# Last feed-forward half of a two-layer diffusion backbone: the first pair of up projections multiplies x·(1 + scale), and the norm's factor and the shift's product are applied to the result

## The chip, the cores and the metric

One Trainium2 chip, one of its cores. The metric is the device time of one execution in microseconds (us); the kernel before has three runs, 1758.97, 1759.12 and 1761.3 us, so a median of 1759.12 us.

## The reference

Two layers work on 256 latent tokens x and 256 context tokens z, 1024 wide. Each layer is a half-step feed-forward, a token mixing and a second half-step feed-forward; the mixing of the last layer gives no context output, and its last feed-forward runs on the latent tokens alone. What the change touches is that last half:

```python
def rms_norm(x):
    return x * lax.rsqrt(jnp.mean(x * x, axis=-1, keepdims=True) + EPS)
def modulate(h, shift, scale):
    return h * (1.0 + scale) + shift
def swiglu(h, w1, w3, w2):
    return (jax.nn.silu(h @ w1) * (h @ w3)) @ w2

x = x + mx[5] * (mix_x @ w_out[l])
x = x + 0.5 * mx[8] * swiglu(modulate(rms_norm(x), mx[6], mx[7]), ffn2_w1[l], ffn2_w3[l], ffn2_w2[l])
```

`mx[6]` and `mx[7]` are the shift and the scale, one number for each of the 1024 features (no dependence on the token). The norm's factor is one number for each token. The hidden width of the feed-forward is 2816, that is 22 blocks of 128.

## The kernel before

**Tiles.** x lies transposed in eight tiles `X[d]`, 128 features by 512 tokens (256 latent, 256 context), fp32. A fp32 product is made of three matmuls of half-precise parts: both operands are split into a high part (a cast) and a low part (the difference), and `mm3` (L281) adds hi·hi, hi·lo and lo·hi into PSUM; all of them are issued from `product`, L272. The activations' parts are `hh{d}` and `hl{d}`, eight pairs from `split_tiles` (L254), the same buffers wherever a normed x or a mixing output is multiplied.

**Weights.** They come from HBM in pieces of 512 KB through the SP queue into `raw` (three buffers). `w_conv` (L228) makes `whi` (ScalarE cast, L235) and `wlo` (VectorE subtract, L238), four buffers each. So the piece after the next four is converted into a buffer that matmuls are still reading, and its cast waits for the last of them.

**The norm.** `norm_square` (L286) squares each X tile as it is written (ScalarE, L288 for d = 0, then L296) and adds the squares into `ss` (GpSimd, L299). `norm_stat` (L306) sums over the features with matmuls by a column of ones (L311, and L313 for the last tile where it was not merged into `ss`), takes the mean on VectorE (`ms`, L319) and the power -1/2 on GpSimd (`rs`, L321). `norm_bcast` (L326) transposes the factor over all partitions into the PSUM tile `pb` (L328). `norm_apply_` (L341) then makes for each d: `htmp` = X·(1+scale)·factor (VectorE, L348), `hh` = cast of htmp + shift (ScalarE, L350), and `hl`: for even d on VectorE (L355), for odd d on GpSimd (L353) after a second pass of ScalarE (L352).

**Lags.** Where both streams are normed, `lag` and `lag2` put the norm's small matmuls five or six products behind (a product is one `mm3`, three matmuls), so that other matmuls run meanwhile. The last half has one stream only: `lag` is None, nothing is merged, and the order on TensorE is output projection, norm, feed-forward.

**The feed-forward** (`ffn`, L385). Each of 22 blocks f has two up projections (`p1`, `p3`: 8 products, so 24 matmuls each), then `finish` makes silu(p1)·p3 and splits it into `gh` and `gl`; the down projections `py` follow. The blocks f = 0 and f = 1 are issued as one group: f = 0 in two PSUM tiles of the kind "M", f = 1 in two of the kind "A" (L404 ff), both called `p13`. A block takes two weight pieces, so f = 0 and f = 1 use four.

**Order.** A scheduler places the instructions of each engine at build time from the dependences and from priorities (`tc.high_priority`, L307, L337 and others); the engines then run their own lists in that order and meet by semaphores. `out_proj` multiplies the mixing outputs `mx` (which lie in the same `hh`/`hl` buffers, columns 0 to 255 where the layer is the last) by the output weights: eight tiles `pyo` of 24 matmuls, each added into X (VectorE, L467) and handed to `norm_square`.

Of the kernel before, what the change touches and what calls it, by code (L numbers as in the profile page):

```python
# [29 lines left out]
PR = 50  # L30
# [38 lines left out]
def tile_backbone(ctx: ExitStack, tc: tile.TileContext, a: dict, out: bass.AP):  # L69
    nc = tc.nc  # L70
# [3 lines left out]
    xp = ctx.enter_context(tc.tile_pool(name="stream", bufs=1))  # L74
# [9 lines left out]
    def small(n, name):  # L84
        return sp.tile([P, n], F32, tag=name, name=name, bufs=2 if name[0] in "de" else 8)
# [12 lines left out]
    X = [xp.tile([P, T], F32, name=f"X{d}") for d in range(KD)]  # L98
# [78 lines left out]
    def mcol(l, m, d, s):  # L177
        return mods[l][:, 8 * m + d, s:s + 1]
# [15 lines left out]
    for l in range(2):  # L194
        ffn_units(l, 1)
        for u in ORDER:
# [6 lines left out]
            elif u in "RNQF":  # L203
                name, n = {"F": ("wfou", 2), "R": ("wgr", 2), "N": ("wna", 6), "Q": ("wgqa", 4)}[u]
# [47 lines left out]


    def split_tiles(d):  # L254
        return (xp.tile([P, T], F32R, tag=f"hh{d}", name=f"hh{d}"),
                xp.tile([P, T], F32R, tag=f"hl{d}", name=f"hl{d}"))

    hooks = []
    gate = [None, False]
# [19 lines left out]
    def mm3(ps, w, k, xh, xl, first, last):  # L279
        wh, wl = w[:2]  # L280
        product(((wh[:, k, :], xh), (wh[:, k, :], xl), (wl[:, k, :], xh)), ps, first, last)  # L281
# [76 lines left out]
    def norm_state(l, m, n):  # L358
# [15 lines left out]
        st["apply"] = apply  # L374
        return st


    def down_order(ns, split):
        tail = split if ns > 1 else 0
# [7 lines left out]
    def ffn(l, m, st, n, pool, npool, bg, after, start=None):  # L387
        ns = n // S
        h = st.setdefault("h", {})
        for f0, f1 in ((0, FA), (FA, NF)):  # L390
            G = {}

            def finish(p1, p3):
                sl = pool.tile([P, T], F32, tag="sl", name="sl", bufs=2)
                nc.scalar.activation(sl[:, :n], p1[:, :n], AF.Silu)
                g = pool.tile([P, T], F32, tag="g", name="g", bufs=2)
                nc.vector.tensor_tensor(out=g[:, :n], in0=p3[:, :n], in1=sl[:, :n], op=ALU.mult)  # L397
                gh = pool.tile([P, T], F32R, tag="gh", name="gh", bufs=FA)
                nc.scalar.copy(gh[:, :n], g[:, :n])
                gl = pool.tile([P, T], F32R, tag="gl", name="gl", bufs=FA)  # L400
                nc.vector.tensor_tensor(out=gl[:, :n], in0=g[:, :n], in1=gh[:, :n].bitcast(F32), op=ALU.subtract)
                G[len(G)] = (gh, gl)
                if f0 or len(G) > (SKIP if start else 0):
                    step(bg)  # L404
                    step(bg)

            fs = list(range(f0, f1))
            if f0 == 0:
                ps, ws = {}, {}
                for f in (0, 1):  # L410
                    for j in range(2):
                        ps[f, j] = bank("M" if f == 0 else "A", "p13")
                steps = [(s, 0, KD) for s in range(ns)]
                if start is not None:
                    steps = [(s, k0, k0 + 2) for k0 in range(0, KD, 2) for s in range(ns)]
                for i, (s, k0, k1) in enumerate(steps):
                    if start is not None:
                        start(s, k0, k1)
                    c = slice(s * S, (s + 1) * S)
                    for f in (0, 1):  # L420
                        for j in range(2):
                            if (f, j) not in ws:
                                ws[f, j] = w_next()
                        for k in range(k0, k1):
                            for j in range(2):
                                mm3(ps[f, j][:, c], ws[f, j], k, h[k][0][:, c], h[k][1][:, c],
                                    i == 0 and k == k0, i == len(steps) - 1 and k == k1 - 1)
                        if i == len(steps) - 1:
                            finish(ps[f, 0], ps[f, 1])
                fs = fs[2:]  # L430
            for f in fs:
                w1 = w_next()
                w3 = w_next()
                p1, p3 = bank("M", "p1"), bank("M", "p3")
                for ps, w in ((p1, w1), (p3, w3)):
                    for k in range(KD):
                        mm3(ps[:, :n], w, k, h[k][0][:, :n], h[k][1][:, :n], k == 0, k == KD - 1)
                finish(p1, p3)
            nk = f1 - f0
            held = {}  # L440
            for mt, s0, s1 in down_order(ns, SPLIT if f1 == NF else 0):
                if mt not in held:
                    if mt == KD - 1 and f1 == NF:
                        lead[0] = ltail[0]
                    held[mt] = [w_next(), w_next()]
                ws = held[mt]
                c = slice(s0 * S, s1 * S)
                py = bank("M", "py")
                for kk in range(nk):
                    mm3(py[:, c], ws[kk // (nk // 2)], kk % (nk // 2), G[kk][0][:, c], G[kk][1][:, c], kk == 0, kk == nk - 1)  # L450
                evac(l, m + 2, mt, py, s0, s1)
                if f1 == NF:
                    after(mt, s0, s1)
                if s1 == ns:
                    step(bg)
                    step(bg)
        for _ in bg:
            pass
# [12 lines left out]
    def mixing(l, st, pool, npool):  # L471
        last = l == 1
# [65 lines left out]
        def gates():  # L538
            wh, wl, wf = w_next()
            pg = mmt("pg")  # L540
            for k in range(KD):
                j = 32 * (k % 4)
                nc.tensor.matmul(pg[j:j + 32, :], wf[:, k, :], h[k][0].bitcast(F32), start=k < 4, stop=4 < k)  # L543
            for k in range(KD):
                nc.tensor.matmul(pg[0:32, :], wh[:, k, :], h[k][1], start=False, stop=k == KD - 1)
            gg = big("gg")
            nc.scalar.copy(gg, pg)
            yield
            g["B"] = [big("Bf"), big("Bb")]
            t1, t2 = [], []  # L550
            for dr in range(2):
                pz = bank("A", "pz")
                nc.tensor.matmul(pz, wg[:, dr, :], gg, start=True, stop=True)
                b_ap = vec[:, l, V_BF + dr:V_BF + dr + 1]
                t1.append(big("t1"))
                nc.scalar.activation(t1[dr], pz, AF.Abs, bias=b_ap)
                t2.append(big("t2"))
                nc.vector.tensor_scalar(out=t2[dr], in0=pz, scalar1=b_ap, scalar2=0.0, op0=ALU.add, op1=ALU.min)
            yield
            last_act = None  # L560
            for fn, kw in ((AF.Exp, dict(scale=-1.0)), (AF.Ln, dict(bias=1.0))):
                for dr in range(2):
                    with tc.issue_after(last_act) if last_act is not None else nullcontext():
                        last_act = nc.scalar.activation(t1[dr], t1[dr], fn, **kw).ins
            for dr in range(2):
                B = g["B"][dr]
                nc.vector.tensor_tensor(out=t2[dr], in0=t2[dr], in1=t1[dr], op=ALU.subtract)
                for c in range(4):
                    o_, i_ = B[:, c * P:(c + 1) * P], t2[dr][:, c * P:(c + 1) * P]
                    if dr:  # L570
                        o_, i_ = o_[:, ::-1], i_[:, ::-1]
                    nc.vector.tensor_tensor_scan(out=o_, data0=ones, data1=i_, initial=0.0, op0=ALU.mult, op1=ALU.add)
# [506 lines left out]
    def out_proj(l, mx, n, after):  # L1079
        ns = n // S  # L1080
        held = {}
        for mt, s0, s1 in down_order(ns, SPLITO):
            if mt not in held:
                if mt == KD - 1:
                    lead[0] = ltail[0]
                held[mt] = w_next()
            c = slice(s0 * S, s1 * S)
            py = bank("M", "pyo")
            for k in range(KD):
                mm3(py[:, c], held[mt], k, mx[k][0][:, c], mx[k][1][:, c], k == 0, k == KD - 1)  # L1090
            evac(l, 5, mt, py, s0, s1)
            after(mt, s0, s1)
# [12 lines left out]
    for l in range(2):  # L1105
# [166 lines left out]
```

## Time and profile before

| | |
|---|---|
| runs, us | 1758.97, 1759.12, 1761.3 (median 1759.12) |
| profiled execution, us | 1757.53, its span 1755.7 |
| granted TensorE clock, mean | 0.989 |
| TensorE busy | 1704.3 us, 97% |
| VectorE, ScalarE, GpSimd busy | 1100.3, 666.7, 214.7 us |
| mixing of the last layer ends, last `pyo` matmul starts | 1555.20 us |
| last half's first `p` matmul starts | 1560.42 us |

Times are in us from the start of the span. The page gives for each engine its busy time; a busy TensorE is not one at its peak, since the records of neighbouring matmuls overlap (each lasts 0.28 us and they start 0.12 us apart). `PEclk` is the clock that TensorE was granted, 1.00 for full speed (2.4 GHz) and 0.50 for half (1.2 GHz). The rows on which the prediction rests stand in a section below.

### The profile page before, as it was taken

Reading aid. Unit: us, or ns where it says so; the run is one execution under the profiler, and the core shown is the slowest. Engines: PE = TensorE matmul, PEld = TensorE weight load, DVE = VectorE, ACT = ScalarE, POOL = GpSimd, SP = SyncE. Lnnn points to the kernel's source line nnn. Section 1 sums busy time; section 2 is a strip of 40 time slices with the busy share of each in tenths; the row PEclk is TensorE's granted clock in tenths of the full one; section 3 lists DMA queues with packets and bytes.
Section 4 is the critical chain, followed back from the end, with each engine's and each line's share of the span. In section 5 each row is a group of like instructions: output and inputs, shape, how many; then the busy total and the mean of one; then the engine's idle time right before and its main releaser. Section 6 shows DMA issues by size and latency. Waiting matters only on the chain.

```text
span 1755.7 us, 28056 instructions
## 1 busy us (share of the span) xinstructions
PE 1704.3 (97%) x11190; PEld 1478.9 (84%) x11190; DVE 1100.3 (63%) x1832; ACT 666.7 (38%) x1122; POOL 214.7 (12%) x249
## 2 busy tenths in 40 slices
PE   7999999998989999999999999999999899989999
PEld 5888888887988788888888888888888787889999
DVE  4577877646787558776333478678733468655554
ACT  4422222235656453222222342222223465554443
POOL 1000000022563130000000210000001335120000
PEclk9999999999999999999999999999999899999999
DMA  9555765334221136555332356567523432146664
GB/s 337 189 185 156 221 208 182 110 97 113 85 56 47 65 104 215 180 177 166 102 96 74 110 203 212 168 199 221 167 81 100 87 108 80 52 130 189 184 191 137
DMA packets 92275, 254.04 MB, mean 145 GB/s; under 512 B 17648, under 2 KB 28144, under 8 KB 91760
## 3 DMA queue, kind: packets, MB, share of 16 engines
q1 hardware_dynamic: 90560, 250.93, 47.6%
q8 instruction: 88, 1.44, 0.3%
q10 hardware_dynamic: 1584, 1.32, 0.2%
q14 instruction: 43, 0.35, 0.1%
HBM read 251.16 MB, written 1.05 MB: 144 GB/s over the span
## 4 chain that ended last, share of the span: by engine, by line
PE 88%; DVE 4%; DMA 2%; ACT 2%; issue 1%; POOL 1%; SPq 0%; POOLq 0%; ACTq 0%
PE p L272 48%; PE py L272 24%; PE pt L272 6%; PE pyo L272 3%; DVE wlo L238 1%; DMA biases<-in_na_rpb_dram 1%; PE po L779 1%; PE prT L770 1%; PE sc L747 1%; PE pf L272 1%; PE modps L143 1%; ACT whi L235 1%; DMA raw<-in_wna_dram 0%; PE pa L663 0%; PE pg L543 0%
## 5 line engine op out<-in xcount | busy, mean ns | idle before, releaser
L235 ACT CAST whi<-raw 128x1024 fp32r<-128x1024 f32 (+3 forms) x358 | 339.9, 951 | 868.3 <-PE p L272 300.2
L238 DVE TENSOR_TENSOR wlo<-raw,whi 128x1024 fp32r<-128x1024 f32 (+3 forms) x358 | 398.4, 1115 | 226.5 <-ACT whi L235 219.8
L272 PE MATMUL p<-hl,whi 128*128 128x512 f32 (+1 forms) x1504 | 528.2, 352 | 2.1 <-DVE hl L355 1.4
L272 PE MATMUL p<-hh,wlo 128*128 128x512 f32 (+1 forms) x1504 | 527.4, 352 | 0.0
L272 PE MATMUL p<-hh,whi 128*128 128x512 f32 (+1 forms) x1504 | 525.9, 353 | 1.1 <-ACT hh L350 1.1
L272 PEld LDWEIGHTS p<-hl,whi 128*128 128x128 f32 x1504 | 285.8, 190 | 40.7 <-DVE hl L355 1.6
L272 PEld LDWEIGHTS p<-hh,whi 128*128 128x128 f32 x1504 | 284.6, 191 | 39.7 <-ACT hh L350 1.6
L272 PEld LDWEIGHTS p<-hh,wlo 128*128 128x128 f32 x1504 | 285.8, 190 | 38.0 <-DVE wlo L238 0.2
L168 DVE CUSTOM_DVE_ANT_0 mprod<-wmod,crow 128x1024 f32<-128x1024 f32 x256 | 301.9, 1219 | 0.0
L272 PE MATMUL py<-gh,whi 128*128 128x512 f32 (+1 forms) x764 | 266.4, 350 | 0.0
L272 PE MATMUL py<-gh,wlo 128*128 128x512 f32 (+1 forms) x764 | 265.8, 348 | 0.0
L272 PE MATMUL py<-gl,whi 128*128 128x512 f32 (+1 forms) x764 | 264.1, 346 | 0.0
L299 POOL TENSOR_TENSOR ss<-ss,sq 128x512 f32<-128x512 f32 (+1 forms) x34 | 40.7, 1198 | 1077.4 <-ACT sq L296 1075.9
L397 DVE TENSOR_TENSOR g<-p,sl 128x512 f32<-128x512 f32 (+1 forms) x88 | 54.9, 624 | 180.4 <-PE p L272 180.0
L272 PEld LDWEIGHTS py<-gh,wlo 128*128 128x128 f32 x764 | 143.4, 188 | 20.5
L272 PEld LDWEIGHTS py<-gl,whi 128*128 128x128 f32 x764 | 143.3, 188 | 19.8
L272 PEld LDWEIGHTS py<-gh,whi 128*128 128x128 f32 x764 | 143.5, 188 | 17.7
L272 PE MATMUL pt<-whi,hl 128*128 128x256 f32 x448 | 132.1, 295 | 7.2 <-POOL hl L353 7.1
L272 PE MATMUL pt<-whi,hh 128*128 128x256 f32 x448 | 132.7, 296 | 0.2
L272 PE MATMUL pt<-wlo,hh 128*128 128x256 f32 x448 | 130.6, 291 | 0.0
L467 DVE SCALAR_TENSOR_TENSOR X<-py,mod,X 128x256 f32<-128x256 f32 x112 | 50.3, 480 | 97.4 <-PE py L272 97.4
L272 PEld LDWEIGHTS pt<-whi,hl 128*128 128x128 f32 x448 | 88.1, 197 | 12.0 <-POOL hl L353 8.9
(218 smaller groups left out, 1714.9 us busy)
## 6 DMA issues: line engine op xcount, KB each, us to landing
wmod<-in_wmodt_dram SPq DMA_DIRECT2D x128, 512.0 KB, 3.9
raw<-in_f1w_dram SPq DMA_DIRECT2D x88, 512.0 KB, 4.3
raw<-in_f2w_dram SPq DMA_DIRECT2D x88, 512.0 KB, 4.2
raw<-in_f1w_dram SPq DMA_DIRECT2D x32, 384.0 KB, 3.7
raw<-in_f2w_dram SPq DMA_DIRECT2D x32, 384.0 KB, 3.2
raw<-in_f1w_dram SPq DMA_DIRECT2D x32, 320.0 KB, 2.9
raw<-in_f2w_dram SPq DMA_DIRECT2D x32, 320.0 KB, 2.9
wfirst<-in_wmodf_dram SPq DMA_DIRECT2D x32, 256.0 KB, 6.5
```

The lines of the kernel that those rows point to most:

```text
L143: nc.tensor.matmul(ps[32 * j:32 * j + 32, :P], sc[:, k, :], tile_[:, j * P:(j + 1) * P], start=(k == 0), stop=(k == KD - 1))
L168: nc.vector.tensor_tensor_reduce(out=prod, in0=raw, in1=crow[:, s], scale=1.0, scalar=0.0, op0=ALU.mult, op1=ALU.add, accum_out=acc[:, s, ...
L235: nc.scalar.copy(hi[:, :k * n], raw[:, :k * n])
L238: wlo[0] = nc.vector.tensor_tensor(out=lo[:, :k * n], in0=raw[:, :k * n], in1=hi[:, :k * n].bitcast(F32), op=ALU.subtract).ins
L272: nc.tensor.matmul(ps, w, x, start=first and i == 0, stop=last and i == len(parts) - 1)
L299: (nc.vector if d == KD - 1 else eng).tensor_tensor(out=st["ss"][:, c], in0=st["ss"][:, c], in1=sq[:, c], op=ALU.add)
L397: nc.vector.tensor_tensor(out=g[:, :n], in0=p3[:, :n], in1=sl[:, :n], op=ALU.mult)
L467: nc.vector.scalar_tensor_tensor(out=X[mt][:, c], in0=py[:, c], scalar=mcol(l, m, mt, s), in1=X[mt][:, c], op0=ALU.mult, op1=ALU.add)
L747: nc.tensor.matmul(ps[:, :n], q[:, e, (t % 2) * P:(t % 2 + 1) * P], ks[e][:, T - n:T], start=i == 0, stop=i == 1)
L770: nc.tensor.transpose(pt[:, c * P:(c + 1) * P], pr[e][:, (2 * half + i) * P:(2 * half + i + 1) * P], ident)
L779: last_mm = nc.tensor.matmul(po[64 * e:64 * e + 64, c0:c0 + P], vs[e][4 - nkt + kt], prT[:, (2 * e + i) * P:(2 * e + i + 1) * P], start=kt ...
```

## The change

Only for the last half (`last`). `st2` takes the mixing's own tiles `mx` as its `hh`/`hl`, lag 5 and lag2 4, and merges the last square. Ahead of the output projection `scaled_shift` puts the split shift into two new columns (512 and 513) of these tiles. After each X tile, `scaled_split` writes the split of x·(1+scale) into columns 256 to 511, which the last layer leaves unused. The pair f = 0 then multiplies columns 256 to 513, that is 256 tokens and twice the shift, before the norm is known. `finish` applies the factor and adds the shift's product to the result. All other blocks multiply the normed values as before, from columns 0 to 255.

```diff
     def split_tiles(d):
-        return (xp.tile([P, T], F32R, tag=f"hh{d}", name=f"hh{d}"),
-                xp.tile([P, T], F32R, tag=f"hl{d}", name=f"hl{d}"))
+        return (xp.tile([P, T + 2], F32R, tag=f"hh{d}", name=f"hh{d}"),
+                xp.tile([P, T + 2], F32R, tag=f"hl{d}", name=f"hl{d}"))
...
+    def scaled_shift(st, l, m):
+        for d in range(KD):
+            hh, hl = st["h"][d]
+            for c in (T, T + 1):
+                nc.scalar.copy(hh[:, c:c + 1], mcol(l, m, d, 0))
+                nc.vector.tensor_tensor(out=hl[:, c:c + 1], in0=mcol(l, m, d, 0), in1=hh[:, c:c + 1].bitcast(F32), op=ALU.subtract)
+
+    def scaled_split(st, l, m, d):
+        hh, hl = st["h"][d]
+        x, c = X[d][:, :S], slice(S, T)
+        with tc.high_priority(offset=PR):
+            nc.scalar.activation(hh[:, c], x, AF.Copy, scale=mcol(l, m + 1, d, 0))
+            nc.vector.scalar_tensor_tensor(out=hl[:, c], in0=x, scalar=mcol(l, m + 1, d, 0), in1=hh[:, c].bitcast(F32),
+                                           op0=ALU.mult, op1=ALU.subtract)
...
-            def finish(p1, p3):
+            def finish(p1, p3, scaled=False):
...
+                if scaled:
+                    rb = pool.tile([P, S], F32, name="rb", bufs=1)
+                    nc.scalar.copy(rb, st["pb", 0][:, :S])
+                    b = small(2, "dsh")
+                    for j, p in enumerate((p1, p3)):
+                        nc.vector.tensor_copy(b[:, j:j + 1], p[:, S:S + 1])
+                        nc.vector.tensor_tensor(out=(sl, g)[j][:, :n], in0=p[:, :n], in1=rb, op=ALU.mult)
+                    nc.scalar.activation(sl[:, :n], sl[:, :n], AF.Silu, bias=b[:, 0:1])
+                    nc.vector.scalar_tensor_tensor(out=g[:, :n], in0=g[:, :n], scalar=b[:, 1:2], in1=sl[:, :n], op0=ALU.add, op1=ALU.mult)
...
                     for f in (0, 1):
+                        scaled = f == 0 and ns == 1
+                        c = slice(S, T + 2) if scaled else slice(s * S, (s + 1) * S)
+                        o = slice(0, T + 2 - S) if scaled else c
...
-            out_proj(l, mx, n2, lambda mt, s0, s1: norm_square(st2, npool, mt, s0, s1, nc.gpsimd))
+            if last:
+                st2.update(h=mx, lag=(5,), lag2=(4,), merge=True)
+                scaled_shift(st2, l, 6)
+
+            def after2(mt, s0, s1):
+                norm_square(st2, npool, mt, s0, s1, nc.gpsimd)
+                if last:
+                    scaled_split(st2, l, 6, mt)
+
+            out_proj(l, mx, n2, after2)
```

In the changed kernel the lines have moved: the shift's split is L381 and L382, the scaled split L388 (ScalarE) and L389 (VectorE), X is written at L494, and `finish` runs from L413 (`rb`) over L416 (`dsh`), L417 (both products by rb), L418 (silu) to L419 (g). The lines up to L328 and L341 to L355 keep their numbers. In the lists below X_82 to X_89 are the eight X tiles, and in the changed kernel the pairs hh_14060/hl_14061, hh_14113/hl_14114, hh_14033/hl_14034 and hh_14037/hl_14038 are those of d = 0 to 3, and hh_14224/hl_14225 that of d = 7.

TensorE, from the end of the output projection on. Before (`p_14587` and `p_14588` are the pair f = 0, `p_14589` and `p_14590` the pair f = 1):

```order
7497 L272 MATMUL pyo<-hl_14225,whi 128x256
7498 L272 MATMUL pyo<-hh_14224,wlo 128x256
7499 L311 MATMUL pb<-ones,ss 128x1
7500 L313 MATMUL pb<-ones,sq 128x1
7501 L311 MATMUL pb<-ones,ss 128x1
7502 L313 MATMUL pb<-ones,sq 128x1
7503 L328 MATMUL pb<-cst,rs 128x128 x2
7504 L272 MATMUL p_14587<-hh_14531,whi 128x256
```

The same place in the changed kernel (`p_14573` and `p_14574` are the pair f = 0, `p_14575` the first tile of f = 1, `p_14576` its second; `p_14777` is the first tile of f = 2):

```order
7528 L272 MATMUL p_14573<-hh_14224,wlo 128x258
7529 L311 MATMUL pb<-ones,ss 128x1 x2
7530 L272 MATMUL p_14574<-hh_14033,whi 128x258
...
7536 L328 MATMUL pb<-cst,rs 128x128 x2
7537 L272 MATMUL p_14574<-hh_14231,whi 128x258
...
7548 L272 MATMUL p_14574<-hh_14224,wlo 128x258
7549 L272 MATMUL p_14575<-hh_14060,whi 128x256
...
7552 L272 MATMUL p_14575<-hl_14061,whi 128x256
...
7558 L272 MATMUL p_14575<-hh_14113,whi 128x256
...
7561 L272 MATMUL p_14575<-hl_14114,whi 128x256
```

Between the last `pyo` matmul and the statistics there are now 30 matmuls of f = 0, between these and the transposes 6, and 12 after the transposes; then f = 1 and the first tile of f = 2 come interleaved.

ScalarE, at the same place. Before:

```order
813 L235 CAST whi<-raw 128x1024
814 L296 ACTIVATE sq<-X_89 128x256
815 L350 ACTIVATE hh_14531<-htmp,mod_98 128x256
816 L350 ACTIVATE hh_14537<-htmp,mod_98 128x256
817 L350 ACTIVATE hh_14544<-htmp,mod_98 128x256
818 L352 ACTIVATE htmp<-htmp,mod_98 128x256
```

In the changed kernel:

```order
827 L235 CAST whi<-raw 128x1024
828 L388 ACTIVATE hh_14224<-X_89,mod_98 128x256
829 L296 ACTIVATE sq<-X_89 128x256
830 L235 CAST whi<-raw 128x1024
831 L350 ACTIVATE hh_14060<-htmp,mod_98 128x256
832 L235 CAST whi<-raw 128x1024
833 L350 ACTIVATE hh_14113<-htmp,mod_98 128x256
834 L350 ACTIVATE hh_14033<-htmp,mod_98 128x256
835 L350 ACTIVATE hh_14037<-htmp,mod_98 128x256
836 L352 ACTIVATE htmp<-htmp,mod_98 128x256 x2
```

Two casts of weights (830 and 832, the fifth and sixth piece of the last half) now stand ahead of the normed tiles; they take the buffers of the two pieces of f = 0, so each waits for one tile of that pair.

VectorE, the same place in the changed kernel:

```order
1543 L299 TENSOR_TENSOR ss<-ss,sq 128x256
1544 L416 COPY dsh<-p_14573 128x1
1545 L319 TENSOR_SCALAR ms<-pb 128x2
1546 L238 TENSOR_TENSOR wlo<-raw,whi 128x1024
1547 L348 SCALAR_TENSOR_TENSOR htmp<-X_82,mod_98,pb 128x256
...
1551 L416 COPY dsh<-p_14574 128x1
1552 L355 SCALAR_TENSOR_TENSOR hl_14061<-htmp,mod_98,hh_14060 128x256
1553 L238 TENSOR_TENSOR wlo<-raw,whi 128x1024
1554 L348 SCALAR_TENSOR_TENSOR htmp<-X_86,mod_98,pb 128x256
```

Here too the fifth and sixth `wlo` stand among the norm's operations (before, none stood between `ms` and the last `hl`), and the last sum of squares is VectorE's.

## Rows read from the trace of the kernel before

**Rows 1.** The page: the busy time of each engine, and the chain that ended last, by engine.
```profile
PE 1704.3 (97%) x11190; PEld 1478.9 (84%) x11190; DVE 1100.3 (63%) x1832; ACT 666.7 (38%) x1122; POOL 214.7 (12%) x249
PE 88%; DVE 4%; DMA 2%; ACT 2%; issue 1%; POOL 1%; SPq 0%; POOLq 0%; ACTq 0%
```
**Rows 2.** Stretches of time, TensorE alone: from and to, length, busy time and matmuls begun, granted clock, DMA share, GB/s.
```profile
1530.00:1541.00 11.00, 9.65 (x86) 1.00 0.00 0
1558.00:1562.00 4.00, 2.01 (x8) 0.71 0.68 214
1562.00:1566.00 4.00, 4.00 (x21) 0.50 0.02 4
1600.00:1700.00 100.00, 100.00 (x841) 1.00 0.63 184
```
**Rows 3.** The chain of waits that ended last, from 1553 to 1600 us: start, length, what.
```profile
1554.59 1.22 POOL ss L299
...
1558.11 0.72 POOL rs L321
...
1558.88 0.45 PE pb L328 x2
...
1559.35 0.49 DVE htmp L348
...
1559.86 0.52 ACT hh L350
...
1560.42 39.64 PE p L272 x305
```
**Rows 4.** Timeline of TensorE: start, length, line, operation, tiles, shapes, count, and in brackets the idle time before it with what ended it.
```profile
1555.20 0.28 PE L272 MATMUL pyo<-hh,wlo 128*128 128x256 f32 x1
...
1557.01 0.38 PE L313 MATMUL pb<-ones,sq 128*128 128x1 f32 x2 [0.77 <-ACT sq L296]
1557.25 0.36 PE L311 MATMUL pb<-ones,ss 128*128 128x1 f32 x2
...
1558.88 0.43 PE L328 MATMUL pb<-cst,rs 128*128 128x128 f32 x2 [1.04 <-POOL rs L321]
1560.42 0.80 PE L272 MATMUL p<-hh,whi 128*128 128x256 f32 x2 [1.11 <-ACT hh L350]
...
1566.10 0.41 PE L272 MATMUL p<-hh,wlo 128*128 128x256 f32 x1
1566.31 0.52 PE L272 MATMUL p<-hh,whi 128*128 128x256 f32 x2
1566.66 0.28 PE L272 MATMUL p<-hl,whi 128*128 128x256 f32 x1
1566.78 0.28 PE L272 MATMUL p<-hh,wlo 128*128 128x256 f32 x1
```
**Rows 5.** Timeline of VectorE, same columns.
```profile
1555.52 0.48 DVE L467 SCALAR_TENSOR_TENSOR X<-pyo,mod,X 128x256 f32<-128x256 f32 x1 [0.30 <-PE pyo L272]
1556.67 1.22 DVE L238 TENSOR_TENSOR wlo<-raw,whi 128x1024 fp32r<-128x1024 f32 x1 [0.67 <-ACT whi L235]
1557.88 0.16 DVE L319 TENSOR_SCALAR ms<-pb 128x2 f32<-128x2 f32 x1
1559.35 1.66 DVE L348 SCALAR_TENSOR_TENSOR htmp<-X,mod,pb 128x256 f32<-128x256 f32 x4 [1.31 <-PE pb L328]
1560.92 0.87 DVE L355 SCALAR_TENSOR_TENSOR hl<-htmp,mod,hh 128x256 fp32r<-128x256 f32 x2
```
**Rows 6.** Timeline of ScalarE, same columns.
```profile
1555.59 1.04 ACT L235 CAST whi<-raw 128x1024 fp32r<-128x1024 f32 x1 [1.15 <-DMA raw<-in_f2w_dram]
1556.55 0.41 ACT L296 ACTIVATE sq<-X 128x256 f32<-128x256 f32 x1
1559.86 1.31 ACT L350 ACTIVATE hh<-htmp,mod 128x256 fp32r<-128x256 f32 x3 [2.90 <-DVE htmp L348]
1561.07 0.49 ACT L352 ACTIVATE htmp<-htmp,mod 128x256 f32<-128x256 f32 x1
...
1570.09 1.05 ACT L235 CAST whi<-raw 128x1024 fp32r<-128x1024 f32 x1 [4.90 <-PE p L272]
```
**Rows 7.** Timeline of GpSimd, same columns.
```profile
1561.64 0.75 POOL L353 TENSOR_TENSOR hl<-htmp,hh 128x256 fp32r<-128x256 f32 x1 [2.82 <-ACT htmp L352]
```
**Rows 8.** The mixing of the last layer: a ScalarE copy of two columns, a wait of TensorE in the output projection, and two TensorE products of 129 and 127 columns, of which the second reads its moving operand from column 129 on.
```profile
1517.03 0.17 ACT L986 COPY fy<-pfo 128x2 f32<-128x2 f32 x1
1539.29 0.61 PE L272 MATMUL pyo<-hh,whi 128*128 128x256 f32 x3 [1.24 <-ACT hh L836]
1516.22 0.39 PE L981 MATMUL pfo<-UC,fou 128*128 128x129 f32 x2
1516.44 0.39 PE L982 MATMUL pfo<-UC,fou 128*128 128x127 f32 x2
```
**Rows 9.** Stretches elsewhere in the kernel: from and to, length, busy time and count of TensorE, of its weight loads, of VectorE, ScalarE and GpSimd, granted clock, DMA share, GB/s.
```profile
395.00:399.00 4.00, 1.81 (x13) 1.40 (x12) 4.00 (x6) 1.78 (x6) 1.35 (x2) 1.00 0.60 129
399.00:403.00 4.00, 3.27 (x15) 3.28 (x16) 2.05 (x5) 1.91 (x5) 2.16 (x3) 0.52 0.71 155
411.00:415.00 4.00, 2.25 (x17) 1.84 (x16) 1.73 (x4) 0.87 (x2) 3.60 (x4) 1.00 0.23 24
415.00:419.00 4.00, 3.98 (x26) 2.80 (x25) 3.02 (x3) 1.60 (x3) 2.13 (x3) 1.00 0.02 4
```

More of the change, by code (lines that the diff above doesn't have):

```diff
@@ L391, in ffn @@
             G = {}
-            def finish(p1, p3):
+            def finish(p1, p3, scaled=False):
                 sl = pool.tile([P, T], F32, tag="sl", name="sl", bufs=2)
-                nc.scalar.activation(sl[:, :n], p1[:, :n], AF.Silu)
                 g = pool.tile([P, T], F32, tag="g", name="g", bufs=2)
-                nc.vector.tensor_tensor(out=g[:, :n], in0=p3[:, :n], in1=sl[:, :n], op=ALU.mult)
+                if scaled:
[7 more added lines that the diff above has]
+                    nc.vector.scalar_tensor_tensor(out=g[:, :n], in0=g[:, :n], scalar=b[:, 1:2], in1=sl[:, :n], op0=ALU.add, op1=ALU.mult)
+                else:
+                    nc.scalar.activation(sl[:, :n], p1[:, :n], AF.Silu)
+                    nc.vector.tensor_tensor(out=g[:, :n], in0=p3[:, :n], in1=sl[:, :n], op=ALU.mult)
                 gh = pool.tile([P, T], F32R, tag="gh", name="gh", bufs=FA)
@@ L418, in ffn @@
                         start(s, k0, k1)
-                    c = slice(s * S, (s + 1) * S)
                     for f in (0, 1):
+                        scaled = f == 0 and ns == 1
+                        c = slice(S, T + 2) if scaled else slice(s * S, (s + 1) * S)
+                        o = slice(0, T + 2 - S) if scaled else c
                         for j in range(2):
@@ L425, in ffn @@
                             for j in range(2):
-                                mm3(ps[f, j][:, c], ws[f, j], k, h[k][0][:, c], h[k][1][:, c],
+                                mm3(ps[f, j][:, o], ws[f, j], k, h[k][0][:, c], h[k][1][:, c],
                                     i == 0 and k == k0, i == len(steps) - 1 and k == k1 - 1)
                         if i == len(steps) - 1:
-                            finish(ps[f, 0], ps[f, 1])
+                            finish(ps[f, 0], ps[f, 1], scaled)
                 fs = fs[2:]
@@ L542, in gates @@
                 j = 32 * (k % 4)
-                nc.tensor.matmul(pg[j:j + 32, :], wf[:, k, :], h[k][0].bitcast(F32), start=k < 4, stop=4 < k)
+                nc.tensor.matmul(pg[j:j + 32, :], wf[:, k, :], h[k][0][:, :T].bitcast(F32), start=k < 4, stop=4 < k)
             for k in range(KD):
-                nc.tensor.matmul(pg[0:32, :], wh[:, k, :], h[k][1], start=False, stop=k == KD - 1)
+                nc.tensor.matmul(pg[0:32, :], wh[:, k, :], h[k][1][:, :T], start=False, stop=k == KD - 1)
             gg = big("gg")
```

## The prediction

> **What bounds the kernel now.** I read the page first: TensorE is busy for 1704.3 of the span's 1755.7 us and holds 88% of the chain that ended last [rows 1], so only time in which TensorE stands still or runs at half clock can be won. Then the stretches of time: from 1600 to 1700 us TensorE is busy for 100.00 of 100 at clock 1.00, while from 1558 to 1562 it is busy for 2.01 of 4 and the next 4 us run at 0.50 [rows 2]. Third, the chain of waits through that place: sum of squares on GpSimd, power, transposes, htmp, hh, and then TensorE with nothing between its products up to 1600 [rows 3]. This is the norm between the last output projection and the last feed-forward, and nothing else is there for TensorE to do.
>
> Its price by TensorE's timeline [rows 4]: the last output matmul begins at 1555.20, the next could begin 0.12 later, at 1555.32 (0.12 is the step at full clock, 1566.66 to 1566.78). The first up projection begins at 1560.42: 5.1 us lost. From there to 1566.31 the step is 0.21 (1566.10 to 1566.31), the half level; 28 matmuls take 5.89 us there where they would take 28 x 0.12 = 3.36 at full clock: 2.5 us lost. Together **7.6 us**. Since TensorE has no gap behind it up to the end, the end moves with the moment at which the first matmuls of the feed-forward are done.
>
> **The change, part by part.** It fills the wait with the 48 matmuls of f = 0, which now need x and the scale, but not the norm. I carry the new order forward with times of the rows of before.
>
> *The 30 matmuls ahead of the statistics.* They run from 1555.32 to 1555.32 + 30 x 0.12 = 1558.92. The two extra columns (258 for 256) cost 48 x 0.12 x 2/256 = 0.05 us. The last three need the split of X7. X7 ends at 1556.00 [rows 5]; ScalarE is then in a weight cast until 1556.63 [rows 6]; the scaled cast, priced as the square of the same shape (0.41 [rows 6]), ends at 1557.04. VectorE is in its weight part until 1557.89 [rows 5], and the low part, priced as an hl (0.87 for two [rows 5]), ends at about 1558.3. The 29th matmul reads it at 1555.32 + 28 x 0.12 = 1558.68. So there is no wait, with 0.4 to spare. The other splits come one per output tile and find both engines with room, though X6 and X7 are then written some 0.4 late; 16 operations of 0.41 to 0.44, at nothing. If that cover were gone, 0.4 us would be lost here.
>
> *Statistics.* The last square is merged by VectorE behind the low part, at about 1558.7, before 1558.92. Two matmuls of 0.24 (1557.01 to 1557.25 [rows 4]) lead to 1559.40; the two of the unmerged square, 0.48, are gone. Then 6 matmuls of f = 0 run to 1560.12. Mean: 0.4 after the last statistic began, as before (from 0.23 behind 1557.25 to 1557.88 [rows 4, 5]), so 1559.56 to 1559.72. The shift's copy ahead of it on VectorE, one column, is priced at 0.17 as ScalarE's two-column copy [rows 8]; it waits for the 30th matmul and is over before the statistics are. Power: 0.07 later, 0.72 long [rows 3], so the transposes begin at 1560.56: TensorE waits 0.45. Transposes: 0.45 [rows 3], to 1561.0; 12 matmuls, to 1562.45. Now f = 0 is done.
>
> *What is queued ahead of the normed tiles.* The change adds a wait here. The fifth weight cast now stands ahead of hh0 on ScalarE and the sixth ahead of hh1; before, the first of them came after everything, at 1570.09 [rows 6]. The fifth waits for the first tile of f = 0 (30th matmul, ended at about 1559.05): cast of 1.05 [rows 6] to 1560.1, VectorE's part of 1.22 [rows 5] to 1561.3. Only then comes htmp0, which could have begun at 1561.03 (0.47 behind the transposes [rows 3]): 0.3 late. Four htmp take 1.66 [rows 5], the first 0.49 [rows 3]; hh0 takes 0.52 [rows 3] and is ready at 1562.3, just before TensorE is free. The sixth cast waits for the second tile of f = 0 (1562.6), and runs to 1563.65 with hh1, hh2, hh3 behind it (1.31 for three [rows 6]), to 1564.9, then the second pass of htmp1 (0.49 [rows 6]), to 1565.3, then GpSimd's hl1 (0.75 [rows 7]), to 1566.1. VectorE ends its four htmp at 1562.96, copies the second shift column, and makes hl0 by 1563.5.
>
> *TensorE there.* Three matmuls on hh0 to 1562.81; wait for hl0, 0.7; six matmuls on hl0 and hh0, three on hh1, to 1564.6; wait for hl1, 1.5. Later low parts come every 0.4 to 0.8 us and find a backlog of f = 1 and f = 2, priced at nothing.
>
> *Sum.* Now lost: 0.47 statistics + 0.45 wait + 0.45 transposes + 0.7 + 1.5 + 0.05 for the columns = **3.6 us**, against 7.6: a gain of 4.0, if the clock holds.
>
> *The rest.* 16 ScalarE and 16 VectorE operations of one column make the shift's split, in the mixing; at 0.17 each [rows 8] 2.7 us on each engine, which in most places only fill idle time: bounds 0 and 0.8 later for TensorE, taken as 0.1. The scheduler also moves some output products forward into the end of the mixing. From 1530 to 1541 TensorE is busy for 9.65 of 11 [rows 2], 1.24 of it one wait of an output product for hh [rows 8]. If this wait is filled, 1.3 us is won; if a product comes later, up to 0.8 is lost; I take 0.5 won, near the middle. The new finish of f = 0 (a copy, two products, a silu with bias, 0.4 us each like the operations above) has read its PSUM tiles by about 1570, behind the norm's low parts; f = 3, the first to need them again, begins behind 144 matmuls, at about 1576: nothing. DMA issues are the same, in the same order on SP. In all -4.0 - 0.5 + 0.1 = -4.4 us.
>
> **Against which time.** The profiled execution took 1757.53, so 1753.1; the median of the runs is 1759.12, 1.6 above it. On the median that is **1754.7 us**.
>
> **The rivals.**
>
> *The clock falls in the new thin stretch.* From 1562 to 1566 my chain has TensorE busy for 0.81 + 1.1 = 1.9 of 4 us. Elsewhere, 1.81 busy of 4 was followed by a granted clock of 0.52, and 2.25 of 4 by 1.00 [rows 9]: this stretch lies between. A fall would cost about what it costs now, 2.5 us, and leave a gain of 1.9: **1757.2**. Against it: the gaps are two, with matmuls between, and the 1.24 us wait at 1539 cost no clock: 1.00 from 1530 to 1541 [rows 2, 8]. The Trainium skill, page "TensorE: Matmul & The Clock Gate", Part 1, says that half speed is the default state and that recent activity lifts it; rows 9 agree, with 0.52 behind the thinner and 1.00 behind the denser stretch, and by that rule this rival depends on the moment at which the thin stretch falls.
>
> *The queue eats the gain.* Normed tiles stand behind two weight conversions. If the fifth and sixth piece land later, or X6 and X7 slip and the scaled split with them, hl1 comes 1.5 to 3 us later than 1566.1, and a gain of 1.4 to 2.9 is left, near **1757**. For it: the change puts 2.3 us of conversion (1.05 and 1.22) ahead of a chain that had none. Against it: TensorE has other products up to 1562.45.
>
> *Slower: the width of the tiles.* All 16 tiles grow to 514 columns, 2056 bytes, so every second one may begin 8 bytes off. The kernel has some 6000 matmuls that read them. If each took 1.3 ns more, 8 us would be lost, the gain gone, and the kernel 3.5 us slower: near **1762.7**; it decides from about 0.7 ns each (no gain left). Against it: a product of 127 columns that starts at column 129 takes no longer (0.39) than one of 129 columns that starts at an even one (0.39) [rows 8]. The Trainium skill, page "Advanced Engine Details and Errata", section SBUF Cachelines, says that SBUF has lines of 16 bytes and that going to another line costs; by that rule a shifted row of 256 columns touches 65 lines for 64, an estimate of 1.9 ns per shifted matmul and some 5 us in all. The trace speaks against it, by the row just named.
>
> *It could also win more.* Were hl1 not late and the 1.24 us wait filled, the gain would be 4.0 + 1.5 + 1.2 = 6.7: 1752.4.
>
> **How the numbers follow.** 0.2% is 3.5 us, about what a measurement of this kernel can tell from no change. My forecast, a gain of 3.6 to 6.7, has 0.56, the clock 0.25, the queue 0.12, the width 0.07. Faster by over 0.2%: the forecast and a little of the next two where the mixing gives its 1.3, 0.61. Within: the clock and the queue, less that, 0.30. Slower: the width and some of what the mixing could lose, 0.09. The range goes from 1752.0 (the larger gain, and half of a microsecond between sets of runs) to 1758.4 (the clock falls and the mixing loses 0.8 more than taken, 1757.2 + 1.2); the forecast's own is 1752.4 to 1755.5.
>
> **What would show it.** Matmuls of 258 columns from about 1555 on with no wait ahead of the first; a wait near 0.45 ahead of the transposes; waits of 0.7 and 1.5 for hl0 and hl1; the fifth cast near 1559 and the sixth near 1562.6; clock 1.00 in every stretch from 1555 to 1575. Half clock near 1566 would make the first rival right; a wait for hl1 of over 3 us the second; a longer mean of the matmuls in the first 1500 us, where nothing else has changed, the third.

## The result and the profile after: 11 us slower, and not where the change works

The changed kernel takes 1770.44 us (median of four runs, 1769.21 to 1771.35) against 1759.05 (four runs, 1758.97 to 1761.3): ratio 1.0066, interval [1.0054, 1.0078]. The forecast was 1754.7 in a range of 1752.0 to 1758.4. It was wrong in sign.

At the place that the change is about, the waits came out nearly as forecast. TensorE's waits there, by line waited for (us in total, times, longest), changed kernel, 1572 to 1592 us:

```profile
PE p L272 <- POOL hl L353: 1.4, 1, 1.4
PE p L272 <- DVE hl L389: 0.6, 1, 0.6
PE p L272 <- DVE hl L355: 0.5, 1, 0.5
PE pb L328 <- POOL rs L321: 0.2, 1, 0.2
```

Forecast were, in this order, 1.5, 0, 0.7 and 0.45. The stretches there (columns as in [rows 2], which they answer):

```profile
1574.00:1578.00 4.00, 3.40 (x28) 1.00 0.74 212
1578.00:1582.00 4.00, 3.33 (x26) 1.00 0.66 190
1582.00:1586.00 4.00, 2.59 (x15) 0.80 0.57 184
1586.00:1590.00 4.00, 4.00 (x29) 0.77 0.03 13
```

TensorE is no longer idle for 5 us, and the clock still falls, for a shorter time: the first rival came true in part. From the start of the last output matmul to that of the last matmul of the kernel it is 192.30 us where it was 196.89, but part of these 4.6 us has another cause (below).

The time went elsewhere. Stretches of before, and then of the changed kernel, in parts of the program where both issue the same matmuls (the last line is from the last half):

```profile
100.00:300.00 200.00, 200.00 (x881) 1.00 0.63 192
700.00:900.00 200.00, 200.00 (x881) 1.00 0.50 152
```
```profile
100.00:300.00 200.00, 200.00 (x865) 1.00 0.62 189
700.00:900.00 200.00, 200.00 (x865) 1.00 0.52 155
1600.00:1700.00 100.00, 100.00 (x855) 1.00 0.66 193
```

TensorE is busy all the time in both, at full clock in both, and begins 865 matmuls where it began 881: a 512-column matmul starts later behind the one before it, and nothing waits. In the last half it is the other way round: 855 for 841 [rows 2], so 256-column matmuls follow each other faster. A busy share of 100% hides both. In groups, from 100 to 300 us (line, operation, out<-in, shapes, count, busy us, mean ns of one), before and then changed:

```profile
L272 PE MATMUL p<-hh,wlo 128*128 128x512 f32 x198 | 77.1, 389 | 0.0
L272 PE MATMUL py<-gl,whi 128*128 128x512 f32 x96 | 37.3, 388 | 0.0
```
```profile
L272 PE MATMUL p<-hh,wlo 128*128 128x512 f32 x193 | 75.8, 393 | 0.0
L272 PE MATMUL py<-gl,whi 128*128 128x512 f32 x96 | 37.9, 394 | 0.0
```

Not only the products of the widened hh/hl are slower, but also py, whose gh/gl the change does not touch. The mean distance between starts in unbroken runs of such matmuls is called the step here: p 226.76 ns before and 231.22 after, py 228.96 and 232.59 (232.4 in five of its six stretches, 233.3 in one); in the last half p 120.0 and 116.7. For 2880 and 1404 matmuls of 512 columns that is 12.8 + 5.1 = 17.9 us. By stage (from starts on TensorE's timeline, us, each against before), with the experiments of below:

| kernel | first feed-forward | mixing and output of layer 0 | its second and the next feed-forward | mixing and output of layer 1 | last half |
|---|---|---|---|---|---|
| changed | +7.2 | +0.4 | +10.2 | -0.2 | -4.6 |
| e1, wide tiles alone | +4.7 | +1.1 | +8.0 | +0.6 | -4.1 |
| e2, what lies behind moved | +2.4 | +1.1 | +2.8 | 0.0 | -0.9 |
| e15, change without shift and width | +3.0 | +1.4 | 0.0 | +2.1 | -3.9 |
| e13, change at aligned places | -0.4 | +2.0 | -3.3 | -2.9 | -1.0 |
| e14, e13 and columns from 112 | -0.6 | +2.5 | -3.3 | -1.9 | -6.1 |

The first feed-forward, which waits for its first loads, and the mixings vary by 2 to 3 us between kernels in which they are the same; the last half varies by the clock and by the 256-column step.

### The profile page after: what moved, and what is told of

Its sections match the earlier page's. It is cut to its first block, busy times and chain, and to the rows that moved or that the text cites. A ratio compares the mean times of both kernels' runs of the same rounds, so it can differ in the third digit from the quotient of the medians.

```text
span 1768.7 us, 28103 instructions
## 1 busy us (share of the span) xinstructions
PE 1714.8 (97%) x11186; PEld 1471.0 (83%) x11186; DVE 1108.3 (63%) x1861; ACT 671.9 (38%) x1147; POOL 213.6 (12%) x249
## 4 chain that ended last, share of the span: by engine, by line
PE 87%; DVE 5%; DMA 4%; ACT 2%; issue 1%; POOL 1%; SPq 0%; POOLq 0%; ACTq 0%
PE p L272 48%; PE py L272 24%; PE pt L272 6%; PE pyo L272 3%; DMA biases<-in_na_rpb_dram 1%; DVE wlo L238 1%; PE po L806 1%; PE prT L797 1%; PE pf L272 1%; PE sc L774 1%; ACT whi L235 1%; DMA raw<-in_wna_dram 0%; PE pa L690 0%; DMA raw<-in_f1w_dram 0%; DMA wfirst<-in_wmodf_dram 0%
## 5 line engine op out<-in xcount | busy, mean ns | idle before, releaser
L272 PE MATMUL p<-hl,whi 128*128 128x512 f32 (+2 forms) x1504 | 530.8, 354 | 4.5 <-POOL hl L353 2.1
L272 PE MATMUL p<-hh,wlo 128*128 128x512 f32 (+2 forms) x1504 | 528.2, 353 | 0.3 <-DVE wlo L238 0.3
L272 PE MATMUL p<-hh,whi 128*128 128x512 f32 (+2 forms) x1504 | 525.8, 353 | 1.0 <-ACT whi L235 0.9
L272 PEld LDWEIGHTS p<-hl,whi 128*128 128x128 f32 x1504 | 283.3, 189 | 48.0 <-POOL hl L353 2.5
L272 PEld LDWEIGHTS p<-hh,whi 128*128 128x128 f32 x1504 | 280.9, 188 | 44.5 <-ACT whi L235 1.1
L272 PEld LDWEIGHTS p<-hh,wlo 128*128 128x128 f32 x1504 | 283.3, 189 | 41.5 <-DVE wlo L238 0.6
L272 PE MATMUL py<-gh,wlo 128*128 128x512 f32 (+1 forms) x764 | 267.7, 351 | 0.0
L272 PE MATMUL py<-gl,whi 128*128 128x512 f32 (+1 forms) x764 | 267.7, 351 | 0.0
L272 PE MATMUL py<-gh,whi 128*128 128x512 f32 (+1 forms) x764 | 267.3, 352 | 0.0
L272 PEld LDWEIGHTS py<-gl,whi 128*128 128x128 f32 x764 | 143.9, 188 | 20.8
L272 PEld LDWEIGHTS py<-gh,wlo 128*128 128x128 f32 x764 | 143.8, 188 | 20.8
L272 PEld LDWEIGHTS py<-gh,whi 128*128 128x128 f32 x764 | 143.7, 188 | 20.9
L272 PE MATMUL pt<-whi,hl 128*128 128x256 f32 x448 | 131.6, 294 | 8.7 <-POOL hl L353 8.6
L272 PE MATMUL pt<-whi,hh 128*128 128x256 f32 x448 | 131.6, 294 | 0.2 <-ACT nt L548 0.2
L272 PE MATMUL pt<-wlo,hh 128*128 128x256 f32 x448 | 130.0, 290 | 0.0
L494 DVE SCALAR_TENSOR_TENSOR X<-py,mod,X 128x256 f32<-128x256 f32 x112 | 50.3, 481 | 103.4 <-PE py L272 103.3
L272 PEld LDWEIGHTS pt<-whi,hl 128*128 128x128 f32 x448 | 87.0, 194 | 13.5 <-POOL hl L353 11.5
```

What stands on the lines that cost most here:

```text
L272: nc.tensor.matmul(ps, w, x, start=first and i == 0, stop=last and i == len(parts) - 1)
L494: nc.vector.scalar_tensor_tensor(out=X[mt][:, c], in0=py[:, c], scalar=mcol(l, m, mt, s), in1=X[mt][:, c], op0=ALU.mult, op1=ALU.add)
```

## The experiments

The theory after the result: a matmul's step depends on where its moving operand (the activations' tile that it streams) lies in SBUF, and the wider tiles moved it. Tiles begin at multiples of 32 bytes, so the 2056 bytes of a tile take 2080, hh/hl drift by 32 from tile to tile, and what lies behind moves by 512, by 576 with the new `dsh`. "At 64" below means the tile's first byte modulo 512. Before, the weights whi/wlo and hh/hl lie at 64, gh/gl at 128.

**e1: wide tiles alone.**
```diff
-        return (xp.tile([P, T], F32R, tag=f"hh{d}", name=f"hh{d}"),
-                xp.tile([P, T], F32R, tag=f"hl{d}", name=f"hl{d}"))
+        return (xp.tile([P, T + 2], F32R, tag=f"hh{d}", name=f"hh{d}"),
+                xp.tile([P, T + 2], F32R, tag=f"hl{d}", name=f"hl{d}"))
...
```


> The kernel before with nothing changed but the width of the 16 hh/hl tiles (514 columns; pitch 2080 bytes, since tiles begin at multiples of 32; what lies behind them moves by 512). Its instructions are those of before in the same order. Theory of the place (the wider tiles move the operands of the matmuls, and the 512-column matmuls take 3 to 4 ns more): 1759 + 4428 x 0.0039 = about 1776, step of p in the first 300 us 0.231 for 0.227. Rival (the time is lost in the last mixing or the last half, by the new order): 1759, step 0.227.

1767.78 against 1757.79 (one run each). p's step is 231.3, as in the changed kernel; py's is 229.0, as before, and 512 is a move that leaves the place modulo 512. So ten microseconds come from the width alone, without one instruction of the change. The 1776 counted py's matmuls too, which kept their step, and left out that 256-column steps fall.

**e2: only what lies behind moved, by 576; e3: all hh/hl moved by 32.**
```diff
+    pad = sp.tile([P, 144], F32, name="pad", bufs=1)     # e2
+    pad = xp.tile([P, 8], F32, name="pad")               # e3, ahead of hh0
+    nc.gpsimd.memset(pad, 0.0)
```


> The kernel before with an unused tile of 576 bytes behind the hh/hl tiles: hh and hl lie as before, everything behind them (gh, gl, the mixing's tiles) lies where the changed kernel has it. If the place of each operand counts by itself: p at 0.2268 as before, py at 0.2323 for 0.2289, so 1404 x 0.0034 = 4.8 us more, about 1764. If only the width of hh/hl counts (and py is slowed by something that hh/hl do): 1759. If only what lies behind counts: about 1776.

> The kernel before with an unused tile of 32 bytes ahead of hh0: all hh/hl and what lies behind move by 32 bytes, pitch 2048 as before. If the place of hh/hl relative to the weights' tiles counts: step of p at or near 0.231, up to 1771. If the pitch alone counts (tiles that lie differently to each other): 1759.

e2: 1762.88, 5.1 more than 1757.79, where 4.8 was expected. e3: 1778.51, so a move by 32 bytes costs 20.7 us, more than the 1771 that was expected at most, and worse than the changed kernel, whose tiles lie at all multiples of 32 in turn. Groups of e2, then of e3, same stretch (L274 is L272, moved by the pad's two lines):
```profile
L274 PE MATMUL p<-hh,wlo 128*128 128x512 f32 x195 | 75.9, 389 | 0.0
L274 PE MATMUL py<-gl,whi 128*128 128x512 f32 x96 | 37.9, 395 | 0.0
```
```profile
L274 PE MATMUL p<-hh,wlo 128*128 128x512 f32 x190 | 75.0, 395 | 0.0
L274 PE MATMUL py<-gl,whi 128*128 128x512 f32 x96 | 38.3, 399 | 0.0
```
Each moving operand's own place counts: e2 slows py alone. The pitch (the distance from one tile to the next) is not needed for it: e3 keeps 2048.

**e4: the change without the shift and without the width** (f = 0 multiplies 256 columns; its shift's product is left out); **e15: the same, timed.**
```diff
-        return (xp.tile([P, T + 2], ...
+        return (xp.tile([P, T], ...
...
-                scaled_shift(st2, l, 6)
...
-                        c = slice(S, T + 2) if scaled else ...
+                        c = slice(S, T) if scaled else ...
```


> The changed kernel without the shift in its pair f = 0: hh/hl are 512 wide again, the pair multiplies 256 columns, and the shift's product is left out of f = 0. Everything else of the change stands. Theory of the place: the local gain stays (4.6 us from the last output product to the end, by the traces) and the loss is gone: about 1754.5. Rival (the order costs the time): about 1770 as the changed kernel.

> The changed kernel without the shift in f = 0 and without wider tiles again (the shift's product of f = 0 is left out), timed, since the single run of it stands against a spread of 2 to 3 us. The change's own part, without any move of tiles: 2.1 us by the shorter waits and up to 2.5 us more where the clock does not fall, 1754.5 to 1757, ratio 0.9975 to 0.999.

One run of 1754.99 against 1757.79, then 1757.17 (eleven runs) against 1759.53: ratio 0.9988 [0.9979, 0.9997]. So the early pair itself, without the shift, gains some 2 us on the median (0.5 to 3.7 by the interval), less than my 4.4. In the profiles of e4 and e15, which are one kernel, the last half is 3.9 us shorter and the clock stays up at the thin stretch; in e13, with the same order on TensorE there and nearly the same waits (0.2, 0.5 and 1.4; in e15 0.2, 0.4 and 1.5), it is followed by 0.57. e15, then e13:
```profile
1569.00:1573.00 4.00, 2.10 (x16) 1.00 0.61 154
1573.00:1577.00 4.00, 4.00 (x34) 1.00 0.28 112
```
```profile
1558.00:1562.00 4.00, 2.24 (x17) 1.00 0.56 146
1562.00:1566.00 4.00, 3.85 (x19) 0.57 0.30 118
```
One order, both outcomes: in the profiles of this order the clock stayed up twice without the shift (e4, e15) and fell twice with it (changed kernel, e13). Whether the shift or chance decides it, and how often the clock fell in the runs without a profile, is not shown.

**e5, e6, e7, e10, e11: other places**, by pads of 448, 480 with 32, 64 with 320, 192 and 320 bytes as in e2 and e3; **e9: all moved together**, weights too:
```diff
+    pad = cp.tile([P, 16], F32, name="pad")              # e9, ahead of the weights' tiles
```


> The kernel before with the hh/hl tiles moved by 448 bytes, so that they begin at 0 modulo 512, and gh/gl at 64 (before: 64 and 128; the weights' tiles stay at 64 modulo 512). If the step depends on the place of the moving operand relative to the weights modulo 512 alone, py now takes the step that p had at 64, 0.2268 (256 columns: 0.120), and p at 0 shows a new one. If it depends on something else (which tile it is, the place modulo more than 512), py takes another step than 0.2268.

> The kernel before with hh/hl at 32 modulo 512 and gh/gl at 128 as before. py: 0.2289 as before whatever the rule. p: above 0.2268 if 64, the weights' own place, is the best for it; all starts tried so far that are 32 off a multiple of 64 (96, 160) took 0.233, so 0.233 is expected, and a time near 1776; 1759 if only distance counts and 32 on this side is harmless.

> The kernel before with hh/hl at 128 modulo 512 and gh/gl at 0. If the place modulo 512 alone counts, p takes the step that py had at 128, 0.2289 (2880 x 0.0021 = 6 us more), and py the step that the run with hh/hl at 0 shows for p.

> The kernel before with an unused tile of 64 bytes ahead of the weights' tiles: all of raw, whi, wlo, X, hh/hl, gh/gl move together by 64, so hh/hl lie at 128 modulo 512 and gh/gl at 192, and the weights at 128 too. If the step depends on the distance to the weights: p at 0.2268, py at 0.2289 as before, 1758. If on the place of the moving operand alone: p at 0.2289, py at 0.2333, as those places had with the weights at 64: about 1758 + 6 + 6 = 1770.

> The kernel before with hh/hl at 256 and gh/gl at 320 modulo 512. Both places are new. If 64 is a best place among equals, p and py take 0.2289 or 0.2333 and the time is 1764 to 1778; a place at which the 512-column step is below 0.2268 would show as a time below 1755.

> The kernel before with hh/hl at 384 and gh/gl at 448 modulo 512, the last two multiples of 64. As for 256 and 320: 1764 to 1778 unless one of the places is better than 64.

Times of e5, e6, e7, e9, e10 and e11: 1767.89, 1776.24, 1763.47, 1761.42, 1768.28 and 1764.69, one run each, against medians of 1758.38 (e5 to e7) and 1758.98. Steps in ns, whichever of p or py stood at the place (weights at 64; 256 columns in the last half):

| place modulo 512 | 0 | 32 | 64 | 96 | 128 | 160 | 192 | 256 | 320 | 384 | 448 |
|---|---|---|---|---|---|---|---|---|---|---|---|
| 512 columns, p | 233.3 | 233.3 | 226.8 | 233.3 | 228.9 | | | 233.3 | | 228.9 | |
| 512 columns, py | 233.3 | | 226.7 | | 229.0 (e6: also 233.3) | 233.3 | 233.3 | | 226.7 | | 232.4 |
| 256 columns, p | 113.3 | 118.3 | 120.0 | 116.7 | 117.8 | | | 117.8, then 113.3 | | 117.8 | |
| 256 columns, py | 117.8 | | 119.9 | | 117.8 | 120.0 | 118.7 | | 119.9 | | 118.7 |

For 512 columns p and py agree to 0.1 wherever both stood at one place, but for e6, and places 256 apart agree to 1 (192 and 448 are the pair that differs). In e9 p kept 226.8 and py 229.0 though they lay at 128 and 192: in this one move of all tiles the distance to the weights counts, not the place itself. Its time is 3 us above the 1758 expected, in the first feed-forward and the mixings (+1.7, +1.5 and +1.4), not in the steps. e9's groups, same stretch:
```profile
L274 PE MATMUL p<-hh,wlo 128*128 128x512 f32 x197 | 76.7, 389 | 0.0
L274 PE MATMUL py<-gl,whi 128*128 128x512 f32 x96 | 37.3, 388 | 0.0
```
The place does not settle the step alone. In e6 gh/gl lie at 128 as before, and 228.9 was expected whatever the rule; two of its six stretches of py take 233.3, the other four 228.9. In e10 the 256-column products of p take 117.8 in the first part of the last half and 113.3 in the second, with hh/hl where they were. e6 in two stretches of py alone, then e10 in two of p alone (matmuls begun in brackets):
```profile
170.00:230.00 60.00, 60.00 (x259) 1.00 0.68 207
1165.00:1225.00 60.00, 60.00 (x264) 1.00 0.70 213
```
```profile
1590.00:1630.00 40.00, 40.00 (x342) 1.00 0.68 203
1685.00:1725.00 40.00, 40.00 (x355) 1.00 0.64 194
```
And for 256 columns p and py differ at place 0 (113.3 and 117.8). What chooses between two steps at one place, these runs do not show.

The kernel before had p at the best place for 512 columns and the worst of these for 256.

**e8: no tile moved, the shift by 32 matmuls of two columns.**
```diff
...
+                                        nc.tensor.matmul(psh[:, 2 * j:2 * j + 2], ws[f, j][q][:, k, :], sh[:, k, :], ...)
```


> The changed kernel with 512-wide tiles as before and the shift's product of f = 0 by 32 small matmuls of two columns (shift's high and low part against whi and wlo) into a PSUM tile of its own. No tile moves. Theory of the place: the first 1370 us as before, the last half shorter than before by the 4 us that the run without the shift gained, less what the 32 small matmuls take and no wait hides (32 x 0.06 to 0.12 = 1.9 to 3.8, of which up to 2 in waits): 1755 to 1758. Rival (the change itself is slower): above 1760.

1758.46 (ten runs) against 1758.38: ratio 1.0001 [0.9991, 1.0011], so nothing is left of the gain. Such a matmul takes a step of 0.11 us, nearly as much as one of 256 columns (0.12 here). Two of them on TensorE's timeline:
```profile
1562.58 0.25 PE L464 MATMUL psh<-dgs,wlo 128*128 128x2 f32 x1
1562.69 0.25 PE L464 MATMUL psh<-dgs,whi 128*128 128x2 f32 x1
```
22 of them lie between 1562.55 and 1564.82; then come the two transposes and 12 matmuls of 256 columns, and among these, at about 1566.4, the clock fell, although TensorE had been busy throughout:
```profile
1562.00:1566.00 4.00, 4.00 (x37) 1.00 0.30 116
1566.00:1570.00 4.00, 4.00 (x22) 0.55 0.47 131
1570.00:1574.00 4.00, 4.00 (x23) 0.60 0.37 99
```

**e12: the kernel before, normed values of the last half in columns 112 to 367.**
```diff
+            if last:
+                st2["col"] = 112
...
+            if "col" in st:
+                hh, hl = hh[:, st["col"]:], hl[:, st["col"]:]
```


> The kernel before with one thing changed: in the last feed-forward half the normed values go into columns 112 to 367 of hh/hl and are read there, so that the 256-column matmuls read from 0 modulo 512 (64 + 448) where they read from 64. No tile moves and no instruction is added. Theory of the place: 1056 matmuls at 0.1133 for 0.1200, 7.0 us less: about 1751.5, ratio 0.996. If the place of the tile and not of the columns counts: 1758.5, ratio 1.000.

1753.22 (ten runs, 1748.27 to 1758.90) against 1758.98: 0.9970 [0.9955, 0.9984], near the 0.996. From 1600 to 1700 us:
```profile
1600.00:1700.00 100.00, 100.00 (x874) 1.00 0.65 192
```
874 matmuls for 841 [rows 2], without an instruction more or less.

**e13: the whole change at aligned places; e14: with columns from 112 as well.**
```diff
...
+        return (xp.tile([P, T + 64], F32R, tag=f"hh{d}", name=f"hh{d}"),
+                xp.tile([P, T], F32R, tag=f"hl{d}", name=f"hl{d}"))
...
+            hi, lo = (st["h"][d][0][:, T + j:T + j + 1] for j in (0, 1))
...
+                    nc.vector.tensor_tensor(out=b, in0=bb[:, 0:4:2], in1=bb[:, 1:4:2], op=ALU.add)
```


> The changed kernel with its tiles placed again: hh 576 columns wide (2304 bytes), hl 512, both shift parts in hh's columns 512 and 513 (high and low, added after the products), small tiles in two buffers for eight to make room; hh and hl lie at the weights' own place modulo 256, and so do gh/gl. If the place alone costs the changed kernel its time: p at 0.2268, py at 0.2267, the first 1375 us 2 to 3 us shorter than before (1404 x 0.0022) and the last half shorter by the change's own gain, 2 to 4.5 us as the clock falls or not: 1751 to 1755, ratio 0.996 to 0.998. If the change has a cost of its own: 1759 or above.

> As the last one, and the normed values of the last half in columns 112 to 367, at 0 modulo 256 against the weights: 1008 matmuls of 256 columns at 0.1133 for 0.1200, 6.7 us less again: 1744 to 1748, ratio 0.992 to 0.994. If overwriting the scaled columns makes the normed tiles wait for f = 0, up to 1 us of it is lost.

e13: 1751.85 (five runs) against 1759.53, ratio 0.9954 [0.9940, 0.9967]. e14: 1748.11 (five runs), ratio 0.9936 [0.9923, 0.9948]. Both are faster than the kernel before and the changed one. e13's groups:
```profile
L272 PE MATMUL p<-hh,wlo 128*128 128x512 f32 x199 | 77.4, 389 | 0.0
L272 PE MATMUL py<-gl,whi 128*128 128x512 f32 x96 | 37.3, 389 | 0.0
```
The change is the same and the hh tiles are even wider than in the changed kernel, but hh/hl and gh/gl all lie at the weights' place modulo 256. In e14 the normed values overwrite scaled columns, and the scheduler then puts the rest of f = 0 behind the first products of f = 1: TensorE waits 1.77 us for the last sum of squares and 1.11 for hh0, and the clock falls as before (0.63 and 0.52 from 1557 to 1565), so part of what the early pair gives is lost again. What e14 has over e13 is the 256-column step (113.4 for 120.0 ns over some 1000 matmuls).

## Why the prediction was wrong

- **What bounds the kernel**, the 5.1 us and 2.5 us of [rows 3, 4]: right but for a count. Between 1560.42 and 1566.31 there are 26 matmuls, not 28, so half clock cost 5.89 - 26 x 0.12 = 2.8 us, and the whole price is 7.9 for 7.6.
- **The chain of the new order**: right but for one wait and some sizes. The low part of X7 was priced at 0.44 with 0.4 us to spare; it was 0.6 late. VectorE was the reason, priced at nothing ("both engines with room"): three of the last four scaled low parts took 0.96, and X7 was written 2.3 us after the last output matmul began where it had been 0.3 [rows 4, 5]. Beside each of the three GpSimd's sum of squares was running, beside the fourth, of 0.47, none; no run tests whether that is the reason. VectorE, then GpSimd, then ScalarE:
```profile
1573.05 1.21 DVE L238 TENSOR_TENSOR wlo<-raw,whi 128x1024 fp32r<-128x1024 f32 x1
1574.18 0.96 DVE L389 SCALAR_TENSOR_TENSOR hl<-X,mod,hh 128x256 fp32r<-128x256 f32 x1
1575.07 0.47 DVE L494 SCALAR_TENSOR_TENSOR X<-pyo,mod,X 128x256 f32<-128x256 f32 x1
1576.59 0.47 DVE L389 SCALAR_TENSOR_TENSOR hl<-X,mod,hh 128x256 fp32r<-128x256 f32 x1
...
1574.12 0.74 POOL L299 TENSOR_TENSOR ss<-ss,sq 128x256 f32<-128x256 f32 x1 [1.68 <-ACT sq L296]
...
1577.54 1.05 ACT L235 CAST whi<-raw 128x1024 fp32r<-128x1024 f32 x1 [1.16 <-PE p L272]
...
1580.96 1.05 ACT L235 CAST whi<-raw 128x1024 fp32r<-128x1024 f32 x1 [0.17 <-PE p L272]
```
  The queue on ScalarE was as forecast: the fifth and sixth cast stand ahead of hh0 and hh1, each some 0.8 us later behind the last output matmul than forecast, mostly by the 0.6.
- **The clock** was a rival with 0.25. It fell in the changed kernel (0.80, 0.77) and in e13 (0.57), not in e4 and e15.
- **The step that failed** is the price of the wider tiles. The sum gave them 0.05 us, for two more columns in 48 matmuls, and left the step of every other matmul in the program as it was. The runs showed 17.9 us in the 512-column matmuls, before 256-column ones gave some back, and 10.0 us in all by the width alone (e1). The rival that doubted this term, "Slower: the width of the tiles", had 0.07: right in direction, wrong in mechanism in three points. It thought of tiles "8 bytes off"; they lie at multiples of 32. It looked at the widened tiles alone, while py lost 5.1 us too. And it dismissed the effect by [rows 8], two products of 129 and 127 columns, which are neither fp32r (the type of hh, hl and the weights' parts) nor 512 wide and have other weights: no row for the case in hand. Its size, 1.3 ns on 6000 matmuls, was 4.5 ns on 2880, 3.6 on 1404 and a gain of 3.3 on some 1000. The Trainium skill's rule that I put beside it (page "Advanced Engine Details and Errata", section SBUF Cachelines, 16-byte lines) does not explain it: no operand here begins off a 16-byte line, and a move by 32 bytes of whole lines costs 20.7 us.
- **Neighbouring gain**: of the last half's 4.6 us, e1 has 4.1 without the change, by the 256-column step and a shorter time at half clock. So the profile of after alone would have credited the change with it. The forecast gain of 4.0 showed at its size only where no tile moved and the clock stayed up (3.9 in e4 and e15).
- **The mixing**, -0.5 + 0.1: -0.2 measured, inside what these stages vary by.

What stays open: why the step depends on the distance between moving operand and weights, modulo 256 bytes as far as tried, and what chooses where one place shows two steps. The runs show steps by place, not a mechanism; 224 and the odd multiples of 32 above it were not tried by themselves.

## What to carry to other kernels

A tile that grows by a few bytes moves every tile behind it; before costing such an edit by its instructions, work out where the operands of the busiest matmuls will lie relative to their weights, and put a pad or a padded width there that keeps it. Compare the count of matmuls begun in stretches in which TensorE is 100% busy: that, and not the busy share, shows a slower step. Do not take a matmul of two columns for a small one: with a weight load of its own it cost 0.11 us here, and with 32 of them the whole gain was gone.

## What the runs showed of the hardware that was not expected

- Steps between 226.7 and 233.3 ns for 512 columns and between 113.3 and 120.0 for 256, by the distance of the moving operand from the weights modulo 256 bytes, as far as tried; for p the best place for one width is the worst measured for the other. In e6 and e10 one place shows two of these steps.
- A matmul of two columns steps by 0.11 us at full clock, behind a weight load of its own, and in e8, with TensorE busy for 4.00 of 4 us, the granted clock of the next 4 us still went to 0.55.
- Of the last four scaled low parts on VectorE, the three that began while GpSimd's sum of squares was running took 0.96 us, the one without it 0.47.
